# The second MLP's down product in Strassen blocks, with weight sums formed in the first MLP, in an fp32 decoder trunk

## The chip, the core and the metric

The kernel runs on one core of one Trainium2 chip. The metric is the device time of one execution in microseconds (us). The kernel before takes 2379.09 us (median of 3 runs, 2379.05 to 2379.59). The engines are PE (TensorE, matrix products), DVE (VectorE), ACT (ScalarE), POOL (GpSimd) and SP (SyncE, which here only starts transfers). Data moves between HBM and SBUF by 16 DMA engines; matrix products land in the eight banks of PSUM.

## What is computed

A trunk of two layers over 16 meta tokens and 256 tokens of width 2048, all in fp32: an RWKV-7 mixer, an MLP, gated linear attention (GLA), a second MLP, and a final norm over the 256 tokens. Only the MLPs and the norm matter here:

```python
def rms_norm(x, g, eps=1e-6):
    return x * lax.rsqrt(jnp.mean(x * x, axis=-1, keepdims=True) + eps) * g

def sq_relu_mlp(x, w1, w2):          # w1: 2048 x 8192, w2: 8192 x 2048
    h = jax.nn.relu(x @ w1)
    return (h * h) @ w2

# for each layer i
h = h + mix_out
h = h + sq_relu_mlp(rms_norm(h, norm_mlp[i]), mlp_w1[i], mlp_w2[i])
# at the end
return rms_norm(h, norm_f)[:, N_META:]
```

## The kernel before

The residual `hres` lies in SBUF feature by feature: 16 tiles of 128 features by 272 tokens. Every fp32 operand is cut into two reduced-precision halves, `hi` and `lo`, and a product is hi·hi + hi·lo + lo·hi. Weights come in chunks of 128x1024 (0.52 MB): SP loads a chunk into `raw`, ACT casts it to `hi` (L140), DVE subtracts to give `lo` (L141), and PE uses it for eight 128x128 blocks. In the MLPs one pool holds three `raw` and two each of `hi` and `lo`, so a chunk's `hi` can be written when PE is done with the chunk two before it.

An MLP (`mlp`) cuts its hidden width of 8192 into four quarters of 2048. `up(b)` makes the 16 rows of a quarter: two chunks each, a product over 16 blocks, then ReLU times the norm's factor (`z`, L272), a square (`s`) and the split into `h`. `down(b)` makes 16 rows of output from a quarter, again two chunks each, and adds them to `hres` (L213). The loop runs up(0), up(1), down(0), up(2), down(1), up(3), down(2), down(3). In the first MLP a product is three matmuls of 272 columns a block (`mm3`, L163 to L165). In the second, with 256 tokens, it is one of 512 columns (weight hi against hi and lo of the tokens) and one of 256 (weight lo against hi): `projws`, L196 and L197. The weights stand still in PE and the tokens stream.

A scheduler orders the instructions of each engine when the kernel is built; what is marked as high priority (the weight loads and their splits, by 2000 steps) is put as early as its buffers allow, and any other instruction goes into the first place at which the engine has nothing earlier in the program that it could do by the scheduler's own clock. The engines then execute in that built order. Parts under `manual_schedule` keep PE's order as written. The `x` tiles of the pool `xp` (16 of 128x2x272) hold operands of the mixers; during the first MLP they are free.

After the second MLP the final norm sums squares over the features with a matmul by ones, takes the factor, multiplies `hres` (already scaled by `norm_f`) and stores it feature by feature, five multiplications on DVE and one on POOL (L1328).

Of the kernel before, what the change touches and what calls it, by code (L numbers as in the profile page):

```python
# [10 lines left out]
F32 = mybir.dt.float32  # L11
F32R = mybir.dt.float32r
AF = mybir.ActivationFunctionType
ALU = mybir.AluOpType
# [16 lines left out]
NC4 = 4  # L31
DECAY = float(np.exp(-0.5))
NORM_EPS = 1e-6
# [21 lines left out]
class Kern:  # L55
# [203 lines left out]
    def mlp(self, layer, x, rstd, hres, off, done):  # L259
        nc, tc, ap = self.nc, self.tc, self.ap  # L260
        n = T - off
        w1, w2 = ap[f"mlp_w1_{layer}"], ap[f"mlp_w2_{layer}"]
        with ExitStack() as es:
            hp = es.enter_context(tc.tile_pool(name=f"hid{layer}", bufs=1, side="right", reuse_waits="tile"))

            def up(b):
                hid = []
                for f in range(KT):
                    src = [w1[b * KT + f, i] for i in range(2)]
                    ps = self.joined(hp, self.projw(src, x)) if n == SEQ else self.proj(src, x, n)  # L270
                    z = self.t(hp, [P, T], "z", 2)[:, :n]
                    nc.vector.scalar_tensor_tensor(out=self.two(z), in0=ps, scalar=0.0, in1=self.two(rstd), op0=ALU.max,  # L272
                                                   op1=ALU.mult)
# [4 lines left out]
                    nc.vector.tensor_tensor(out=ht[:, 1, :n], in0=s, in1=ht[:, 0, :n].bitcast(F32), op=ALU.subtract)  # L278
                    hid.append(ht)
                return hid  # L280

            def down(b, hid):
                for f in range(KT):
                    src = [w2[f, 2 * b + i] for i in range(2)]
                    one = n != SEQ or (b, f) == (NHB - 1, KT - 1)
                    self.addto(hres[:, f, off:], [self.proj(src, hid, n)] if one else self.projw(src, hid))
                    if b == NHB - 1:
                        done(f)

            hid = up(0)  # L290
# [4 lines left out]
            down(NHB - 1, hid)  # L295


    def rwkv(self, done):
# [691 lines left out]
        with tc.manual_schedule(engines={ENG.PE}):  # L990
# [5 lines left out]
            for g in range(2):  # L996
                last = nothing
                if g:
# [7 lines left out]
                    last = norm(1)  # L1006
                until(MARK[2 * g])
                some(inv, 99)
# [270 lines left out]
@with_exitstack  # L1279
def trunk(ctx, tc, ap):  # L1280
    K = Kern(ctx, tc, ap)
    nc = tc.nc
    out, hres = ap["out"], K.hres
    st = {}

    def operand(gname, off, pool):
        def f(kt):
            if kt == 0:
                p = pool()
                st["x"] = [K.t(p, [P, 2, T], "x", KT, F32R) for _ in range(KT)]  # L1290
                st["acc"] = K.t(K.sp, [P, T], "acc")
            with tc.high_priority(offset=3000) if kt == KT - 1 else ExitStack():
                K.prep(K.sp, kt, hres[:, kt, off:], gname, st["x"][kt], st["acc"], T - off)
        return f

    def x2():
        K.x2p = K.sp = ctx.enter_context(tc.tile_pool(name="x2", bufs=1, side="right", reuse_waits="tile"))
# [9 lines left out]
    def last(kt):  # L1307
        if kt == 0:
            st["acc"] = K.t(K.sp, [P, T], "acc")
        h = hres[:, kt, NMETA:]  # L1310
        if kt < KT - 1:
            K.sqacc(K.sp, kt, h, st["acc"], SEQ)
        else:
            st["sq"] = K.t(K.sp, [P, T], "sq")[:, :SEQ]
            nc.scalar.activation(st["sq"], h, AF.Square)  # L1315
        nc.scalar.mul(h, h, K.vec("norm_f", kt))

    fp = ctx.enter_context(tc.tile_pool(name="fin", bufs=1, side="right"))
    fin = K.t(fp, [P, KT - 2, SEQ], "fin")
    K.mlp(1, st["x"], rstd, hres, NMETA, last)  # L1320
    ss = K.pm()[:, :SEQ]
    for i, x in enumerate((st["acc"][:, :SEQ], st["sq"])):
        nc.tensor.matmul(ss, K.ones, x, start=i == 0, stop=i == 1)  # L1323
    rstd = K.rstd_from(K.sp, ss, SEQ, 1.0 / D, NORM_EPS, "acc")
    for a, b in ((0, 1), (14, 16), (1, 3), (3, 6), (6, 10), (10, 14)):
        h = hres[:, a:b, NMETA:]
        y = fin[:, a:b] if b < KT else h
        (nc.gpsimd if b == KT else nc.vector).tensor_tensor(out=y, in0=h, in1=rstd.unsqueeze(1).to_broadcast([P, b - a, SEQ]),  # L1328
                                                           op=ALU.mult)
        nc.sync.dma_start(out[:, a:b], y)  # L1330


def _tiles(w):
    k, f = w.shape
    return np.ascontiguousarray(w.reshape(k // 1024, 8, P, f // P, P).transpose(3, 0, 2, 1, 4)).reshape(
        f // P, k // 1024, P, 1024)


def _pad(w, cols):
# [82 lines left out]
```

## Time and profile before

| | |
|---|---|
| Median of three runs | 2379.09 us |
| Profiled execution: span from first to last instruction | 2375.3 us |
| Mean granted PE clock | 0.998 |
| Packets of the one queue that moves data (SP's) | 156784, 446.11 MB, 57.8% of 16 engines' span |
| First MLP, from its first matmul to its last | 590 to 1303 us |
| GLA | 1303 to 1692 us |
| Second MLP | 1692 to 2363 us |

The page gives no duration of the profiled execution other than its span; the median is 3.8 us longer. The span is the part that the trace explains. In groups of instructions, a matmul's duration is modelled and includes the time that it spends in the pipeline, so matmuls overlap; what one costs is the distance from its start to the next one's. The share of DMA is the mean busy share of the 16 DMA engines. Idle time of an engine says who was waited for (`<-`).

### The profile page before, as it was taken

How to read it: one execution, taken by the hardware profiler on the slowest of the kernel's cores; microseconds unless marked ns; L12 is line 12 of the kernel's file. 1: busy time of each engine (PE TensorE's matmuls, PEld its weight loads, DVE VectorE, ACT ScalarE, POOL GpSimd, SP SyncE). 2: the span in 40 equal slices, each digit the busy share in tenths (PEclk: the TensorE clock that was granted, in tenths of full speed). 3: DMA queues.
4: the chain of work that ended last, by engine and by line, in shares of the span. 5: the costliest groups of instructions: out<-in, count | busy, mean ns of one | idle time of the engine just before them, and what ended most of it. 6: DMA issues, size and time to landing. Idle time of an engine off the chain costs nothing. (4 is left out here: it accounts for less than half of the span.)

```text
span 2375.3 us, 48373 instructions
## 1 busy us (share of the span) xinstructions
PE 2344.9 (99%) x19849; PEld 2224.1 (94%) x19849; DVE 1607.3 (68%) x2701; ACT 1259.7 (53%) x2005; POOL 13.6 (1%) x38
## 2 busy tenths in 40 slices
PE   9999999999999999999999999999999999999998
PEld 8888888889999999999999999999999999999997
DVE  8869986848555555555556777767666666666666
ACT  6478645566555345345345556645555445445444
POOL 0000000000000000000000000000000000000000
PEclk9999999999999999999999999999999999999999
DMA  6469754535555555555555655456565666666664
GB/s 214 155 198 310 245 159 145 144 98 180 186 192 189 188 194 187 189 192 188 190 191 190 199 175 174 162 168 202 179 203 200 200 203 200 200 203 200 199 204 169
DMA packets 157005, 449.20 MB, mean 189 GB/s; under 512 B 33968, under 2 KB 49968, under 8 KB 156784
## 3 DMA queue, kind: packets, MB, share of 16 engines
q1 hardware_dynamic: 156784, 446.11, 57.8%
q8 instruction: 156, 2.56, 0.5%
q14 instruction: 65, 0.53, 0.1%
HBM read 429.93 MB, written 14.42 MB: 187 GB/s over the span
## 5 line engine op out<-in xcount | busy, mean ns | idle before, releaser
L141 DVE TENSOR_TENSOR lo<-raw,hi 128x1024 fp32r<-128x1024 f32 (+1 forms) x818 | 927.4, 1140 | 532.9 <-ACT hi L140 523.1
L140 ACT CAST hi<-raw 128x1024 fp32r<-128x1024 f32 (+1 forms) x818 | 794.2, 978 | 918.8 <-PE pj L164 519.4
L163 PE MATMUL pj<-x,hi 128*128 128x272 f32 (+1 forms) x2560 | 728.1, 284 | 1.6 <-DVE r L300 0.9
L165 PE MATMUL pj<-x,lo 128*128 128x272 f32 (+1 forms) x2560 | 714.8, 279 | 5.1 <-DVE lo L141 5.0
L164 PE MATMUL pj<-x,hi 128*128 128x272 f32 (+1 forms) x2560 | 713.8, 279 | 0.5 <-DVE x L240 0.5
L163 PEld LDWEIGHTS pj<-x,hi 128*128 128x128 f32 x2560 | 484.8, 189 | 14.1 <-issue 6.5
L165 PEld LDWEIGHTS pj<-x,lo 128*128 128x128 f32 x2560 | 484.9, 189 | 7.8 <-DVE lo L141 7.5
L164 PEld LDWEIGHTS pj<-x,hi 128*128 128x128 f32 x2560 | 485.0, 189 | 3.2 <-issue 1.4
L196 PE MATMUL pj<-x,hi 128*128 128x512 f32 x1280 | 419.8, 382 | 0.1
L197 PE MATMUL pj<-x,lo 128*128 128x256 f32 x1280 | 348.7, 273 | 0.0
L196 PE MATMUL pj<-h,hi 128*128 128x512 f32 x1008 | 330.3, 382 | 0.0
L163 PE MATMUL pj<-h,hi 128*128 128x272 f32 (+1 forms) x1040 | 290.1, 279 | 0.0
L164 PE MATMUL pj<-h,hi 128*128 128x272 f32 (+1 forms) x1040 | 290.1, 279 | 0.0
L165 PE MATMUL pj<-h,lo 128*128 128x272 f32 (+1 forms) x1040 | 290.1, 279 | 0.0
L197 PE MATMUL pj<-h,lo 128*128 128x256 f32 x1008 | 274.9, 273 | 0.1
L196 PEld LDWEIGHTS pj<-x,hi 128*128 128x128 f32 x1280 | 241.9, 189 | 33.9 <-DVE x L1088 0.4
L197 PEld LDWEIGHTS pj<-x,lo 128*128 128x128 f32 x1280 | 245.8, 192 | 0.1
L196 PEld LDWEIGHTS pj<-h,hi 128*128 128x128 f32 x1008 | 190.5, 189 | 26.5
L163 PEld LDWEIGHTS pj<-h,hi 128*128 128x128 f32 x1040 | 196.6, 189 | 0.0
L164 PEld LDWEIGHTS pj<-h,hi 128*128 128x128 f32 x1040 | 196.6, 189 | 0.0
L165 PEld LDWEIGHTS pj<-h,lo 128*128 128x128 f32 x1040 | 196.6, 189 | 0.0
L197 PEld LDWEIGHTS pj<-h,lo 128*128 128x128 f32 x1008 | 193.5, 192 | 0.4 <-DVE lo L141 0.4
(283 smaller groups left out, 2171.5 us busy)
## 6 DMA issues: line engine op xcount, KB each, us to landing
raw<-mlp_w_d SPq DMA_DIRECT2D x512, 512.0 KB, 3.4
raw<-gla_in_d SPq DMA_DIRECT2D x98, 512.0 KB, 3.4
raw<-w_rkv_d SPq DMA_DIRECT2D x80, 512.0 KB, 4.1
raw<-gla_o_d SPq DMA_DIRECT2D x32, 512.0 KB, 3.3
raw<-w_r_d SPq DMA_DIRECT2D x16, 512.0 KB, 3.4
raw<-rw_oQ_d SPq DMA_DIRECT2D x16, 512.0 KB, 3.4
raw<-lora_d SPq DMA_DIRECT2D x8, 512.0 KB, 3.7
raw<-rw_oA_d SPq DMA_DIRECT2D x8, 512.0 KB, 4.2
```

Source lines behind the costliest of these rows:

```text
L140: nc.scalar.copy(hi[:, h], raw[:, h])
L141: nc.vector.tensor_tensor(out=lo[:, h], in0=raw[:, h], in1=hi[:, h].bitcast(F32), op=ALU.subtract)
L163: nc.tensor.matmul(out, hi[:, ws], xh, start=first, stop=False)
L164: nc.tensor.matmul(out, hi[:, ws], xl, start=False, stop=False)
L165: nc.tensor.matmul(out, lo[:, ws], xh, start=False, stop=last)
L196: nc.tensor.matmul(wide, hi[:, ws], xt, start=kt == 0, stop=False)
L197: nc.tensor.matmul(one, lo[:, ws], xt[:, 0], start=False, stop=kt == nk - 1)
```

## The change

The first MLP's arithmetic and its PE order stay. Four things are new.

**Weight sums.** In the first MLP, `differences` forms three sums of 128x512 blocks of the second MLP's `w2` for 48 sets (4 quarters, 2 halves of the output width, 6 of 8 block rows) and stores them in HBM as `diff`. A set is three fetches by POOL's queue into free `x` tiles, three DVE instructions and three stores by POOL's queue. `paced` hands the steps out over 120 of the 128 rows of the first MLP, one call of `next(pre)` after each row.

**Strassen units.** The second product of the second MLP is turned round: tokens stand still in PE (128 hidden x 128 tokens), weights stream, 512 columns at a time. A unit is a block row p: 256 hidden, 256 tokens, 1024 outputs, or eight block products, of three matmuls each. In the six block rows of `FAST` they become seven products after Strassen (in Winograd's form), which need sums of the hidden blocks (four DVE additions of 128x128 for a pair of rows) and of the weights: a chunk of two `w2` blocks, one of two `diff` blocks, one of a block of each, and a 128x512 difference formed on the spot (`raw4`) with its own split. The eight products go to eight PSUM banks (`own`), which are emptied after the sixth fast row and in the plain rows.

**Order.** Rows of the first product alternate with units, in an order written by hand for PE. The pool `hid1` adds two more `raw`, `hi` and `lo`, used in turn with the old ones.

**Residual and norm.** `hres` is turned to token-by-feature form by 32 PE transposes beside the first eight rows (`htok`), the sums are added to it there, and the final norm works on it directly: squares with a running sum on ACT, factor per token, DVE and ACT scaling by quarters, eight stores.

```diff
+FAST = [0, 1, 2, 4, 5, 6]
...
                     hid.append(ht)
+                    next(pre, None)
...
+            if layer == 0:
+                pre = self.paced(self.differences(), 2 * NHB * KT - 8)
...
+    def differences(self):
...
+        def fetch(u):
...
+            for x, k in zip(held[u], (0, 3, 2)):
+                nc.gpsimd.dma_start(x, w[:, k])
+
+        def form(u):
+            x11, x12, x22 = held[u]
+            tt = nc.vector.tensor_tensor
+            tt(out=x22, in0=x22, in1=x12, op=ALU.subtract)
+            tt(out=x12, in0=x12, in1=x11, op=ALU.subtract)
+            tt(out=x11, in0=x11, in1=x22, op=ALU.add)
+
+        def store(u):
...
+            for x, k in ((t1, 0), (t3, 1), (t2, 2)):
+                nc.gpsimd.dma_start(self.diff[b, g, i][:, k], x)
+
+        def step(u):
+            if u >= 3:
+                store(u - 3)
+            if u < len(units):
+                fetch(u)
+            if 2 <= u < len(units) + 2:
+                form(u - 2)
...
+        def down(b, g):
...
+            def product(at, X, hi, lo, ws, last, first=False):
+                wh, wl, o = self.weave(hi[:, ws]), self.weave(lo[:, ws]), self.pairs(own[at])
+                nc.tensor.matmul(o, X[0], wh, start=first or at not in begun, stop=False)
+                nc.tensor.matmul(o, X[0], wl, start=False, stop=False)
+                nc.tensor.matmul(o, X[1], wh, start=False, stop=last)
...
+                    A = load([(both, w[:, :2])])
+                    B = load([(both, d[:, 1:])])
+                    E = load([(one, w[:, 2]), (two, d[:, 0])])
+                    with tc.high_priority(offset=2000):
+                        r4 = self.t(hp, [P, 512], "raw4", 1)
+                        tt(r4, A[0][:, two], B[0][:, two], ALU.subtract)
+                        G = split(hp, r4, 512)
...
+                    for i in (6, 7, 5, 2, 3, 4, 1) if p == 0 else (1, 6, 7, 5, 2, 3, 4):
+                        product(i, *todo[i], p == FAST[-1] and i in (1, 5, 6, 7))
...
+                unit = down(b, 0)
+                for f in range(10, 16):
+                    next(unit)
+                    up(b, f)
+                for _ in unit:
+                    pass
+                unit = down(b, 1)
+                for f in range(8):
+                    if b < NHB - 1:
+                        up(b + 1, f)
+                    next(unit)
+                for _ in unit:
+                    pass
```

Before each quarter's `down(b, 0)` ten of its rows are done, so each quarter has units 0 to 5 with a row behind each, units 6 and 7 without, then eight units with a row of the next quarter ahead of each; in the last quarter these eight have none.

What stands on DVE in the first MLP's first quarter, before. `lo` is the second half of a chunk, `z` and `h` belong to the 16 hidden rows:

```order
L141 TENSOR_TENSOR lo_8357<-raw_8354,hi_8356 128x1024
L272 SCALAR_TENSOR_TENSOR z_8346<-pj_8285,acc_8279 128x272
L141 TENSOR_TENSOR lo_8387<-raw_8384,hi_8386 128x1024
L278 TENSOR_TENSOR h_8350<-s_8348,h_8350 128x272
L141 TENSOR_TENSOR lo_8425<-raw_8422,hi_8424 128x1024
L272 SCALAR_TENSOR_TENSOR z_8414<-pj_8353,acc_8279 128x272
```

The same engine in the first MLP's second quarter, where the rows are the same, now (L143 is the old L141, L274 and L280 the old L272 and L278; L334 to L336 are the three instructions of a set, on `x` tiles that POOL fetched):

```order
L143 TENSOR_TENSOR lo_9438<-raw_9435,hi_9437 128x1024
L336 TENSOR_TENSOR x_12845<-x_12845,x_12847 128x512
L274 SCALAR_TENSOR_TENSOR z_9427<-pj_9366,acc_8282 128x272
L143 TENSOR_TENSOR lo_9468<-raw_9465,hi_9467 128x1024
L280 TENSOR_TENSOR h_9431<-s_9429,h_9431 128x272
L334 TENSOR_TENSOR x_12983<-x_12983,x_12982 128x512
L335 TENSOR_TENSOR x_12982<-x_12982,x_12981 128x512
L336 TENSOR_TENSOR x_12981<-x_12981,x_12983 128x512
L143 TENSOR_TENSOR lo_9518<-raw_9515,hi_9517 128x1024
L274 SCALAR_TENSOR_TENSOR z_9495<-pj_9434,acc_8282 128x272
L334 TENSOR_TENSOR x_13181<-x_13181,x_13180 128x512
L143 TENSOR_TENSOR lo_9548<-raw_9545,hi_9547 128x1024
```

Between two `lo` there now stand up to three instructions of a set. The scheduler has drawn the sets far ahead of the rows to which `paced` tied them: five stand before the first MLP's first `lo`s, the 6th to the 47th between the 3rd and the 64th of its 256 `lo`s, and the 48th near its end.

POOL's queue in the same stretch, now (it issued no transfer before); `w_d` is `w2`, and the numbers of the `x` tiles tell the sets apart:

```order
L329 DMA x_11005<-w_d 128x512
L329 DMA x_11006<-w_d 128x512
L329 DMA x_11007<-w_d 128x512
L342 DMA diff_8288<-x_10672 128x512
L342 DMA diff_8288<-x_10673 128x512
L342 DMA diff_8288<-x_10671 128x512
L329 DMA x_11141<-w_d 128x512
L329 DMA x_11142<-w_d 128x512
L329 DMA x_11143<-w_d 128x512
L342 DMA diff_8288<-x_10870 128x512
L342 DMA diff_8288<-x_10871 128x512
```

POOL alternates the fetches of a set with the stores of the set two or three before it. A store waits for DVE, and the fetches behind it wait with it.

DVE in the second MLP, before, one row of the first product after the other:

```order
L141 TENSOR_TENSOR lo_24817<-raw_24814,hi_24816 128x1024
L207 TENSOR_TENSOR cj_24781<-pj_24736,cj_24781 128x256
L272 SCALAR_TENSOR_TENSOR z_24784<-cj_24781,acc_21664 128x256
L141 TENSOR_TENSOR lo_24850<-raw_24847,hi_24849 128x1024
L278 TENSOR_TENSOR h_24788<-s_24786,h_24788 128x256
```

and now, beside rows that alternate with fast units (`raw_4084` and `lo_4086` are the difference formed on the spot and its `lo`, `F` and `HS` the sums of hidden blocks and their `lo`):

```order
L209 TENSOR_TENSOR cj_26379<-pj_22261,cj_26379 128x256
L409 SCALAR_TENSOR_TENSOR z_26382<-cj_26379,acc_22244 128x256
L356 TENSOR_TENSOR raw_4084_26508<-raw_26489,raw_26495 128x512
L356 TENSOR_TENSOR lo_26492<-raw_26489,hi_26491 128x1024
L356 TENSOR_TENSOR lo_26463<-raw_26460,hi_26462 128x1024
L356 TENSOR_TENSOR lo_26498<-raw_26495,hi_26497 128x1024
L356 TENSOR_TENSOR lo_4086_26511<-raw_4084_26508,hi_4085_26510 128x512
L356 TENSOR_TENSOR F_26296<-F_26296 128x128 x3
L356 TENSOR_TENSOR lo_26505<-raw_26501,hi_26504 128x1024
L356 TENSOR_TENSOR HS_26389<-F_26296,HS_26389 128x896
```

Where a row had two `lo` and three smaller instructions, a row with its unit now has five `lo`, two half-size instructions for the difference, and the sums of hidden blocks beside the smaller ones.

More of the change, by code (lines that the diff above doesn't have):

```diff
@@ L288, in down @@
                         done(f)
+                    next(pre, None)
+            pre = iter(())
+            if layer == 0:
+                pre = self.paced(self.differences(), 2 * NHB * KT - 8)
             hid = up(0)
@@ L295, in mlp, with operands, paced @@
             down(NHB - 1, hid)
+    def operands(self, b, g, p):
+        return self.ap["w2"][b, g, p]
+    def paced(self, steps, n):
+        steps = list(steps)
+        done = 0
+        for i in range(n):
+            while done < (i + 1) * len(steps) // n:
+                steps[done]()
+                done += 1
+            yield
+    def differences(self):
+        nc = self.nc
+        self.diff = self.t(self.dp, [NHB, 2, len(FAST), P, 3, 512], "diff")
+        units = [(b, g, i) for b in range(NHB) for g in range(2) for i in range(len(FAST))]
+        held = {}
+        def fetch(u):
+            b, g, i = units[u]
+            w = self.operands(b, g, FAST[i])
+            held[u] = [self.t(self.xp, [P, 2, T], "x", KT, F32R).bitcast(F32).rearrange("p s t -> p (s t)")[:, :512]
+                       for _ in range(3)]
+            for x, k in zip(held[u], (0, 3, 2)):
[7 more added lines that the diff above has]
+        def store(u):
+            b, g, i = units[u]
+            t2, t1, t3 = held.pop(u)
+            for x, k in ((t1, 0), (t3, 1), (t2, 2)):
[7 more added lines that the diff above has]
+                form(u - 2)
+        return [lambda u=u: step(u) for u in range(len(units) + 3)]
@@ L1296, in x2 @@
     def x2():
-        K.x2p = K.sp = ctx.enter_context(tc.tile_pool(name="x2", bufs=1, side="right", reuse_waits="tile"))
+        K.sp = ctx.enter_context(tc.tile_pool(name="sp", bufs=1, side="right", reuse_waits="tile"))
+        st["x2"] = ExitStack()
+        K.x2p = st["x2"].enter_context(tc.tile_pool(name="x2", bufs=1, side="right", reuse_waits="tile"))
         return K.x2p
@@ L1305, in trunk @@
     rstd = K.accstd(K.sp, st["acc"], SEQ)
[L1307 to L1330, printed above, removed]
+    st["x2"].close()
+    K.mlp1(st["x"], rstd)
 def _tiles(w):
@@ L1336, in _tiles, with _blocks @@
         f // P, k // 1024, P, 1024)
+def _blocks(w):
+    w = w.reshape(NHB, KT // 2, 2, P, 2, 2, 256, 2).transpose(0, 4, 1, 3, 2, 5, 7, 6).reshape(NHB, 2, KT // 2, P, 4, 512)
+    out = np.empty_like(w)
+    for p in range(KT // 2):
+        out[:, :, p] = w[:, :, p][..., [0, 2, 3, 1], :] if p in FAST else w[:, :, p]
+    return out
 def _pad(w, cols):
@@ L1415 @@
           for k, v in arr.items()}
-    ap["out"] = nc.dram_tensor("out_d", (P, KT, n), F32, kind="ExternalOutput").ap()
+    ap["out"] = nc.dram_tensor("out_d", (2, P, D), F32, kind="ExternalOutput").ap()
     with _tile.TileContext(nc) as tc:
@@ L1419 @@
     r = _run(nc, [{k + "_d": v for k, v in arr.items()}], core_ids=[0])
-    o = r.results[0]["out_d"].transpose(1, 0, 2).reshape(D, n).T
-    return np.ascontiguousarray(o)[None]
+    return np.ascontiguousarray(r.results[0]["out_d"]).reshape(1, n, D)
```

171 lines of the change are left out of this document (170 added, 1 removed).

## The prediction

> **What bounds the kernel now.** I read the page's busy times first, then a table by stretch for the two MLPs, then the order of time inside each.
>
> ```profile
> span 2375.3 us, 48373 instructions
> PE 2344.9 (99%) x19849; PEld 2224.1 (94%) x19849; DVE 1607.3 (68%) x2701; ACT 1259.7 (53%) x2005; POOL 13.6 (1%) x38
> ```
>
> TensorE (PE) is busy for 99% of the span, so a change gains what it takes off PE and loses every moment in which PE waits. POOL does next to nothing. The stretches below are: the first MLP, the second MLP, a piece of the second, and the two spells in which DMA worked hardest.
>
> ```profile
> core 0: us, PE busy (x) PEld busy (x) DVE busy (x) ACT busy (x) POOL busy (x), PEclk, DMA share, GB/s
> 590.00:1303.00 713.00, 712.50 (x6148) 712.17 (x6146) 405.93 (x483) 329.81 (x420) 0.00 (x0) 1.00 0.58 190
> 1692.00:2364.00 672.00, 671.72 (x4114) 617.30 (x4112) 441.08 (x590) 344.47 (x481) 0.00 (x0) 1.00 0.60 198
> 1800.00:2000.00 200.00, 200.00 (x1224) 183.81 (x1223) 131.13 (x176) 102.27 (x144) 0.00 (x0) 1.00 0.61 201
> 196.00:216.00 20.00, 19.77 (x174) 17.93 (x174) 18.02 (x45) 16.71 (x33) 1.07 (x3) 1.00 0.98 337
> 4.00:12.00 8.00, 6.47 (x23) 3.83 (x22) 4.35 (x11) 3.82 (x7) 0.00 (x0) 1.00 1.02 408
> ```
>
> Both MLPs are PE-bound at full clock (PEclk 1.00). In the first, VectorE (DVE) has 307 us to spare and the 16 DMA engines are busy for 0.58 at 190 GB/s. When all 16 are busy all the time they move 408 GB/s; a rate of 190 at a share of 0.58 would be 328 GB/s at full share. These two numbers decide the forecast.
>
> **PE work in the second MLP.** A pair of matmuls, 512 and 256 columns wide, in order of time:
>
> ```profile
> 1899.73 0.38 PE L196 MATMUL pj<-h,hi 128*128 128x512 f32 x1
> 1899.95 0.27 PE L197 MATMUL pj<-h,lo 128*128 128x256 f32 x1
> 1900.06 0.38 PE L196 MATMUL pj<-h,hi 128*128 128x512 f32 x1
> 2363.22 0.28 PE L165 MATMUL pj<-h,lo 128*128 128x256 f32 x1
> ```
>
> The second column is a modelled length; the cost is the distance between starts: 0.22 us for 512 columns, 0.11 for 256. The 200 us stretch has 1224 matmuls, 612 pairs, so 0.327 us a pair and, by thirds, 0.218 us for 512 columns. The second product now takes 63 x 16 pairs, 329.6 us, and a last row of 48 matmuls at 0.112 (5.4 us): 335.0 us. After, it is eight passes of six Strassen units (7 x 3 matmuls) and two plain ones (8 x 3), 174 matmuls each: 1392 x 0.218 = 303.5 us. The first product keeps its 1024 pairs. That is 31.5 us less. Added are 32 transposes of hres. The nearest row is
>
> ```profile
> L732 PE MATMUL pm<-cst,hres 128*64 128x128 f32 x128 | 9.2, 279 | 0.5 <-ACT hres L895 0.5
> ```
>
> whose 279 ns is again a length: 8.9 us at most; 128 columns at the rate above would be 1.8. I take 3.5, as lengths here run two to three times the distance. **PE: -28 us** (-30 to -23).
>
> **The end.** PE's last product ends near 2363.3, and 12 us follow, much of it the five multiplications and the last transfers:
>
> ```profile
> 2366.15 5.23 DVE L1328 TENSOR_TENSOR fin<-hres,acc 128x256 f32<-128x256 f32 x5 [2.19 <-ACT acc L232]
> 2366.20 1.50 POOL L1328 TENSOR_TENSOR hres<-hres,acc 128x512 f32<-128x512 f32 x1 [1867.29 <-ACT acc L232]
> 2366.66 0.34 SPq L1330 DMA_DIRECT2D out_d<-fin  x1
> 2368.27 3.47 SPq L1330 DMA_DIRECT2D out_d<-fin  x4
> ```
>
> After, one addition and one square (0.7 each) follow the last product, two tiny activations, then two DVE and two ScalarE (ACT) scalings side by side, 1.4 us, and transfers. I put it at 7 us: **-5 us** (-7 to 0).
>
> **Weight sums in the first MLP.** Each of 48 sets is three fetches, three DVE instructions and three stores, each of 128x512 fp32 (0.262 MB). The code paces them over 120 of 128 rows. The built order doesn't: of 48 sets, DVE's order holds the 6th to the 47th between the 3rd and the 64th lo of the first MLP, that is 42 sets in 61 chunks of weights out of 256. What a chunk takes:
>
> ```profile
> 902.53 1.05 ACT L140 CAST hi<-raw 128x1024 fp32r<-128x1024 f32 x1 [1.73 <-PE pj L164]
> 903.61 1.23 DVE L141 TENSOR_TENSOR lo<-raw,hi 128x1024 fp32r<-128x1024 f32 x1 [0.52 <-ACT hi L140]
> 904.75 0.44 DVE L278 TENSOR_TENSOR h<-s,h 128x272 fp32r<-128x272 f32 x1
> 905.31 1.05 ACT L140 CAST hi<-raw 128x1024 fp32r<-128x1024 f32 x1 [0.95 <-PE pj L164]
> ```
>
> From hi to hi it is 2.78 us, PE's time for 24 matmuls; 61 chunks are 169.6 us. There are two hi and two lo buffers, so PE can run one chunk ahead of DVE and no more. DVE executes in order: a set's first subtraction waits for its fetch, and behind it stand the next chunk's lo, and behind that PE.
>
> Bytes in these 61 chunks: 42 x 6 x 0.262 = 66.1 MB for the sets, 61 x 0.524 = 32.0 MB of weights, 98.1 MB. Off that come about three sets fetched ahead and three not yet stored (POOL's order puts the fetch of a set behind the store of the third one before it): 4.7 MB. The other 93.4 MB in 169.6 us would be 551 GB/s. At 408 they take 229 us (+59), at 328 they take 285 us (+115). POOL's transfers need the same 16 engines. With two queues full the rate should beat 328; the stretch from 196 us, full as well, speaks against 408 with its 337. I take 365: 256 us, **+86 us** (+59 to +115).
>
> The Trainium skill, "DMA: Bandwidth & Descriptors", section "Issuing engines are not separate DMA queues", says that transfers started from several engines run on the same 16 DMA engines and that this saves issue time alone; its section "Specifications" gives a ceiling of 435 GB/s, by which the term would be +45 us (an estimate). The trace shows 408 at a share of 1.02; no run here has a second queue.
>
> DVE alone would hardly bind:
>
> ```profile
> L141 DVE TENSOR_TENSOR lo<-raw,hi 128x1024 fp32r<-128x1024 f32 x690 | 845.0, 1225 | 520.0 <-ACT hi L140 511.3 <-DMA cad<-ca 2.1
> L141 DVE TENSOR_TENSOR lo<-raw,hi 128x512 fp32r<-128x512 f32 x128 | 82.4, 684 | 12.9 <-ACT hi L140 11.8
> L272 DVE SCALAR_TENSOR_TENSOR z<-pj,acc 128x272 f32<-128x272 f32 x64 | 28.3, 442 | 38.1 <-PE pj L165 38.0
> ```
>
> 61 x 1.225 + 30.5 x (0.44 + 0.44) + 42 x 3 x 0.684 = 188 us in 169.6: at most +18, less since neighbours overlap (904.75 starts 0.09 before 903.61 + 1.23 ends). It lies beside the DMA wait and is not added. Five sets stand before the first MLP, 15 instructions of 0.684: 0 to 10 us; I take **+4**.
>
> **Waits in the second MLP.** A Strassen unit needs three chunks and a 512-wide difference with its own hi and lo, where the same weights were two chunks. DVE, with the durations above (128x512: 0.684) and these:
>
> ```profile
> L272 DVE SCALAR_TENSOR_TENSOR z<-cj,acc 128x256 f32<-128x256 f32 x64 | 27.2, 425 | 2.2
> L207 DVE TENSOR_TENSOR cj<-pj,cj 128x256 f32<-128x256 f32 x64 | 26.7, 418 | 0.0
> ```
>
> 304 lo (372 us), 96 half-size (66), 64 x 0.84 for the rows (54), 96 additions of 512 (66), and the hidden sums, interpolated, about 59: 617 us beside PE's 642, where it was 441 in 672. For a row with a fast unit PE needs 16 x 0.327 + 21 x 0.218 = 9.8 us and DVE 10.5 by lengths, about 9.4 with overlap. 38 such pairs cost 0 to 25 us. The last eight units have no row beside them (PE 4.6 us each, DVE 4.9 to 6), nor have units 7 and 8 of each quarter's first pass: 5 to 35 us more, since behind a waiting lo stand the additions that empty the PSUM banks. I take **+22 us** (+5 to +60). The extra weights cost nothing beside that: 304 x 0.524 = 159 MB in 642 us are 248 GB/s, under 328, and PE's matmuls cover them.
>
> **Sum.** 2375.3 - 28 - 5 + 86 + 4 + 22 = 2454.3 us of span. The median shown is 3.8 us above the profiled span, which I add: **2458 us**, slower by 3.3%.
>
> **Rivals.**
> *The sums stay hidden* (faster). If they ran as paced, 75.5 MB over 713 us would add 106 to 190 GB/s, 296, under both rates, and 98 us of DVE fits in 307. Then 2379 - 33 + 22 = 2368, or 2351 if the second MLP waits for 5 us only. For it: the pacing in the code. Against it: DVE and POOL execute in their built order, 42 sets in 61 chunks. It decides if DMA can move 551 GB/s, or if the sets are not due so early. Chance 0.06, a part of it within 0.2%.
> *POOL's issue binds.* POOL issues no DMA before, so its price isn't shown. SyncE's issue is 0.34 us above, POOL's own instruction 1.50: six a set are 2.0 to 9.0 us, against 6.1 that the forecast has for a set and its chunks (256 / 42). Over 1.02 us each, POOL is the bound; at 1.25 a set takes 7.5 us, 315 us in all, +145, so 2517; at 1.5, 2580. Chance 0.15.
> *DVE locks POOL out.* Should an issue wait for a whole lo and a subtraction, 1.9 us, a set takes 11.4 us, +309: 2681. Chance 0.02. The Trainium skill, "SBUF — State Buffer", section "Who interferes with whom", describes such a lock against descriptors written by GpSimd, but infers that a two-input tensor_tensor doesn't hold it; no run here shows either.
> *The second MLP saturates DVE* beyond my +60, with the rest as forecast: about 2510. Chance 0.05.
>
> **How the numbers follow.** The forecast has 0.72. With all its terms at their good ends it gives 2379 - 37 + 59 + 5 = 2406, at their bad ends 2379 - 23 + 115 + 10 + 60 = 2541. The range 2405 to 2545 leaves out the hidden case, the lock and half of the POOL case. A measurement of this kernel tells 0.2% (5 us) from no change. Faster by more 0.05, within it 0.03, slower 0.92.
>
> **What would show it.** The first quarter or third of the first MLP should have DMA near a share of 1 at 330 to 410 GB/s, PE idle with lo named as releaser, and lo or a subtraction waiting for a transfer; the rest of that stage should run at 2.78 us a chunk. The stage should last about 800 us. If DMA stands below 0.8 there while POOL is busy, the POOL rival holds. The second MLP should have 512-wide matmuls 0.22 us apart, DVE over 85%, and last 655 to 670 us. The forecast is wrong if DMA moves over 450 GB/s, or if the sets wait for nothing.

## The result and the profile after

The changed kernel takes **2616.77 us** (median of 4 runs, 2613.74 to 2621.70), the one before 2379.27: a ratio of 1.1002, 95% interval 1.0987 to 1.1018. It is slower, as forecast, but by 237 us where 79 were forecast, and outside the range. The profiled execution took 2621.7 us with a span of 2619.9.

The page after: its first rows, then two of its rows by slices of 65 us (the granted clock in tenths of full speed, and what the DMA engines moved):

```profile
span 2619.9 us, 48317 instructions
PE 2413.9 (92%) x19205; PEld 2239.0 (85%) x19205; DVE 1832.4 (70%) x3025; ACT 1335.9 (51%) x2075; POOL 167.9 (6%) x325
PEclk9999999998999999999999999999998989989899
GB/s 210 154 234 281 220 137 160 88 248 351 393 391 382 229 190 191 189 192 187 192 200 206 178 168 163 171 200 199 198 198 199 202 165 215 200 182 196 186 209 159
```

PE was busy for 99% of the span and is now busy for 92%, though it has 644 instructions fewer; and its busy time has grown, because the granted clock is no longer full everywhere. The DMA rate stands out in four slices early in the first MLP. In the second MLP (the last third), where most of the time went, nothing stands out in it. The stages, each from the matmul that closes one norm to the one that closes the next, from the traces (the changed kernel's final norm has no such matmul, so there PE's last product ends the second MLP):

| stage, us | before | after | change | forecast |
|---|---|---|---|---|
| RWKV layer | 593.6 | 606.9 | +13.3 | +4 (sets ahead of the first MLP) |
| first MLP | 713.1 | 793.7 | +80.6 | +86 |
| GLA layer | 387.2 | 387.9 | +0.7 | 0 |
| second MLP | 670.9 | 819.4 | **+148.5** | **-6** (PE -28, waits +22) |
| end | 10.6 | 12.1 | +1.5 | -5 |
| span | 2375.3 | 2619.9 | +244.6 | +79 |

The table by stretch of the changed kernel (the part of the first MLP with the sets, the rest of it, the second MLP):

```profile
core 0: us, PE busy (x) PEld busy (x) DVE busy (x) ACT busy (x) POOL busy (x), PEclk, DMA share, GB/s
593.00:858.00 265.00, 211.44 (x1588) 204.83 (x1588) 190.67 (x279) 99.78 (x145) 136.30 (x253) 0.92 1.00 380
858.00:1408.00 550.00, 547.35 (x4719) 546.51 (x4718) 311.06 (x364) 245.38 (x300) 4.15 (x8) 1.00 0.59 195
1786.00:2608.00 822.00, 708.92 (x3475) 609.48 (x3474) 582.48 (x767) 415.06 (x541) 0.00 (x0) 0.93 0.59 193
```

The first row is what was forecast: DMA full, at 380 GB/s. The third is not: DVE is busy for 582 of 822 us (71%), ACT for 415, DMA for 0.59. No engine and no queue is full there, and still PE stands idle for 113 us. The matmul clock is 0.93, because it is halved for 119.5 us of this stage (41.0 us in the first MLP; 0 in both before). PE is busy in 105 of the 119.5 us, and at half rate half of that is lost. So 113 + 52 = 165 us of the second MLP is idleness and slow clock, most of the 177 us that it takes over the forecast 642 us of PE work.

The waits of the changed kernel in its second MLP that bear on loads, on the difference and on PE (engine, what it began late, the releaser; then us in total, times, the longest):

```profile
DVE lo L356 <- ACT hi L380: 127.0, 99, 4.5
ACT hi L380 <- DVE raw L356: 82.5, 32, 8.2
ACT hi L380 <- DMA raw<-mlp_w_d: 53.4, 21, 6.4
PE pj L448 <- DVE cj L209: 37.9, 10, 4.5
DVE raw L356 <- DMA raw<-w_d: 37.2, 16, 4.3
PE pj L405 <- DVE cj L209: 29.5, 12, 4.2
```

They form a ring. DVE waits for ACT's hi, ACT for a subtraction of DVE (`raw`, the difference formed on the spot), and that for a load. And a load is issued the moment DVE gives a buffer back, as the rows of the SyncE queue say:

```profile
SPq L374 <- DVE lo L356: 485.7, 205, 12.0
SPq L374 <- DVE cj L209: 110.0, 48, 3.0
```

What such a wait does to PE, at one place: a plain unit of the third quarter, in order of time on ACT, DVE and PE.

```profile
2240.33 1.04 ACT L380 CAST hi<-raw 128x1024 fp32r<-128x1024 f32 x1 [2.76 <-DMA raw<-mlp_w_d]
2241.28 0.37 ACT L208 COPY cj<-pj 128x256 f32<-128x256 f32 x1
...
2241.40 1.23 DVE L356 TENSOR_TENSOR lo<-raw,hi 128x1024 fp32r<-128x1024 f32 x1 [0.22 <-ACT hi L380]
2242.55 0.68 DVE L356 TENSOR_TENSOR htok<-htok,hres 128x512 f32<-128x512 f32 x1
2243.15 0.42 DVE L209 TENSOR_TENSOR cj<-pj,cj 128x256 f32<-128x256 f32 x1
...
2240.09 0.38 PE L450 MATMUL pu<-hi,HC 128*128 128x512 f32 x1
2243.62 0.79 PE L448 MATMUL pj<-hi,HC 128*128 128x512 f32 x1 [3.16 <-DVE cj L209]
2244.21 0.63 PE L449 MATMUL pj<-lo,HC 128*128 128x512 f32 x1
2244.64 0.63 PE L450 MATMUL pj<-hi,HC 128*128 128x512 f32 x1
```

A load is late by 2.76 us. The copy that empties PE's bank `pj` needs nothing of that load, but it stands behind the cast that does, and `cj` stands behind two more instructions of DVE. PE, which wants `pj` for product 0, stops for 3.16 us. Then its 512-wide matmuls start 0.43 us apart instead of 0.22, until about 2249.7: the clock has halved.

### The profile page after: what moved, and what is told of

It reads as the page before. It is cut to its first block, busy times and chain, and to the rows that moved or that the text cites. A ratio compares the mean times of both kernels' runs of the same rounds, so it can differ in the third digit from the quotient of the medians.

```text
span 2619.9 us, 48317 instructions
## 1 busy us (share of the span) xinstructions
PE 2413.9 (92%) x19205; PEld 2239.0 (85%) x19205; DVE 1832.4 (70%) x3025; ACT 1335.9 (51%) x2075; POOL 167.9 (6%) x325
## 5 line engine op out<-in xcount | busy, mean ns | idle before, releaser
L142 ACT CAST hi<-raw 128x1024 fp32r<-128x1024 f32 (+1 forms) x562 | 526.2, 947 | 638.8 <-PE pj L166 494.4
L143 DVE TENSOR_TENSOR lo<-raw,hi 128x1024 fp32r<-128x1024 f32 (+1 forms) x562 | 613.2, 1100 | 286.5 <-ACT hi L142 282.6
L380 ACT CAST hi<-raw 128x1024 fp32r<-128x1024 f32 (+1 forms) x352 | 339.3, 986 | 313.7 <-DVE raw L356 82.5
L356 DVE TENSOR_TENSOR lo<-raw,hi 128x1024 fp32r<-128x1024 f32 (+1 forms) x352 | 394.5, 1148 | 130.0 <-ACT hi L380 129.0
L405 PE MATMUL pj<-x,hi 128*128 128x512 f32 x896 | 323.0, 406 | 46.4 <-DVE cj L209 29.5
L165 PE MATMUL pj<-h,hi 128*128 128x272 f32 x1024 | 285.8, 279 | 1.0 <-ACT hi L142 1.0
L167 PE MATMUL pj<-h,lo 128*128 128x272 f32 x1024 | 285.9, 279 | 0.8 <-DVE lo L143 0.8
L166 PE MATMUL pj<-h,hi 128*128 128x272 f32 x1024 | 285.7, 279 | 0.0
L406 PE MATMUL pj<-x,lo 128*128 128x256 f32 x896 | 257.0, 287 | 5.1 <-DVE lo L356 4.9
L165 PEld LDWEIGHTS pj<-h,hi 128*128 128x128 f32 x1024 | 193.5, 189 | 1.2 <-ACT hi L142 1.2
L167 PEld LDWEIGHTS pj<-h,lo 128*128 128x128 f32 x1024 | 193.5, 189 | 1.1 <-DVE lo L143 1.0
L166 PEld LDWEIGHTS pj<-h,hi 128*128 128x128 f32 x1024 | 193.5, 189 | 0.0
L342 POOL DMA_DIRECT2D diff<-x x144 | 78.3, 545 | 534.6 <-DVE x L334 464.4
L329 POOL DMA_DIRECT2D x<-w_d x144 | 77.9, 542 | 129.7 <-DMA diff<-x 56.4
```

Of the source, the lines that this page charges most:

```text
L142: nc.scalar.copy(hi[:, h], raw[:, h])
L143: nc.vector.tensor_tensor(out=lo[:, h], in0=raw[:, h], in1=hi[:, h].bitcast(F32), op=ALU.subtract)
L165: nc.tensor.matmul(out, hi[:, ws], xh, start=first, stop=False)
L166: nc.tensor.matmul(out, hi[:, ws], xl, start=False, stop=False)
L167: nc.tensor.matmul(out, lo[:, ws], xh, start=False, stop=last)
L329: nc.gpsimd.dma_start(x, w[:, k])
```

## The experiments

Sixteen runs follow, each of one execution but for the last; the kernel before took 2377 to 2381 us beside them. "Second MLP" and the other names are the stages of the table above. Where the code of a stage stayed as it was, the stage still moved: the second MLP took 812 to 823 us in the runs that left it alone and 833 and 834 in the two that read `w2` in place of `diff` in it, the first MLP 789 to 797. So a difference of less than 10 us between two runs says little. First, which part of the change costs what.

**No weight sums.**

```diff
-            if layer == 0:
-                pre = self.paced(self.differences(), 2 * NHB * KT - 8)
-                    d = self.diff[b, g, FAST.index(p)]
+                    d = w[:, 1:]
```

> Left out: the weight sums of the first MLP; the second MLP reads blocks of w2 in place of diff, in the same sizes and number. Theory (the sums cost what the first MLP and the stage before it gained, 81 + 13 us, and the second MLP's loss is its own): the first MLP back at 713 us, the second unchanged at 819 +-10, the whole near 2616 - 94 = 2522 us. Rival (the two losses belong together, for instance by where diff lies in HBM): the second MLP falls by more than 20 us too.

2545.94 us. The first MLP is back at 713.8 us and the RWKV layer at 595.7, so the sums cost 80 + 11 us there. The second MLP takes 833.9 us. That is 14 us more than in the changed kernel, outside the 10 that were expected, and not less. Its loss is its own: it doesn't come from the sums, from where they lie in HBM or from anything that the first MLP leaves behind.

**The sets' transfers without their arithmetic.**

```diff
-            if 2 <= u < len(units) + 2:
-                form(u - 2)
```

> Left out: the three DVE instructions of each set; fetches and stores stay, so diff holds plain blocks. Theory (PE lost time because DVE, in its built order, stood before a set's transfer with the next lo behind it): the transfers run as fast as the engines let them, nobody on DVE waits, the first MLP is 713 to 735 us and the whole 2530 to 2550. Rival (the transfers themselves starve the weight loads of DMA): the first MLP stays above 770 us.

2575.61 us; first MLP 751.5, between the two theories. The transfers alone cost 38 us of that stage, though DMA is just as full. A stretch of 50 us in this run, where PE is busy for 46 of them:

```profile
700.00:750.00 50.00, 45.95 (x377) 44.04 (x376) 25.03 (x31) 22.73 (x32) 24.89 (x46) 1.00 1.02 407
```

The same stretch of the changed kernel has PE busy for 41 and a clock of 0.93:

```profile
700.00:750.00 50.00, 40.95 (x312) 39.73 (x312) 36.99 (x52) 18.49 (x25) 27.05 (x51) 0.93 1.02 395
```

So full DMA engines are half of the loss in the first MLP. The other half needs DVE's subtractions, which wait for fetches with the next `lo` behind them. In the changed kernel, from 590 to 870 us:

```profile
DVE x L334 <- DMA x<-w_d: 59.8, 31, 4.9
PE pj L167 <- DVE lo L143: 52.0, 28, 4.7
```

**The sets held back to their rows.** A small copy on POOL makes each fetch wait for the row to which `paced` tied it.

```diff
+                    self.mark = s[:, :4]
...
+                    self.mark = hres[:, f, off : off + 4]
...
+                nc.gpsimd.tensor_copy(x[:, :4], self.mark)
                 nc.gpsimd.dma_start(x, w[:, k])
```

> Before each fetch POOL copies four columns of the row just made into the tile that is fetched, which ties each set to its row; the built order then has 48 sets over 220 of 256 chunks. Theory (42 sets in 61 chunks asked for 551 GB/s): about 296 GB/s, DMA under a share of 0.9, the first MLP at 713 to 730 us, the whole near 2616 - 85 = 2530. Rival (each set costs its wait wherever it stands, some 2 us): the first MLP stays above 770 us.

2782.57 us; first MLP 969.5 and halved clock for 174 us of it. Slower still, by 176 us of that stage. The fetches now come row by row, but on DVE the subtraction of a set is still placed where the scheduler took its data to be there. In this trace one `lo` or none starts between the last fetch of a set and its first subtraction. In the first MLP:

```profile
DVE x L337 <- DMA x<-w_d: 186.5, 48, 4.9
PE pj L167 <- DVE lo L143: 168.3, 49, 4.8
```

Each of the 48 sets stops DVE for about 4 us, and PE stops with it.

**The subtractions held back as well.** A value of a later row goes into the first of the three instructions as a scalar, so that DVE's order has a set two steps behind its fetch.

```diff
+            tick = self.t(self.tp, [P, 1], "tick", 2)
+            nc.vector.tensor_scalar(out=tick, in0=self.mark[:, :1], scalar1=0.0, scalar2=1.0, op0=ALU.mult, op1=ALU.add)
-            tt(out=x22, in0=x22, in1=x12, op=ALU.subtract)
+            nc.vector.scalar_tensor_tensor(out=x22, in0=x22, scalar=tick, in1=x12, op0=ALU.mult, op1=ALU.subtract)
```

> As the paced kernel, and a set's first subtraction multiplies by a 1.0 made from the row of two steps later, so that it stands some nine chunks behind the row that its fetch is tied to. Latency theory (the paced kernel lost 4 us on DVE per set, because the build put each subtraction a chunk or two behind a fetch that takes 7.7 us to land, and PE's clock halved behind each stop): no wait for transfers, the first MLP at 715 to 745 us. Rival (DVE's own work in a full order stops PE): above 800 us.

2618.46 us; first MLP 804.6. DVE's waits for fetches are gone, and with them the loss of the run before; still the stage is 11 us longer than in the changed kernel. What is waited for now, in the first MLP, is weights:

```profile
ACT hi L142 <- DMA raw<-mlp_w_d: 181.5, 57, 5.1
PE pj L167 <- DVE lo L143: 32.8, 45, 0.9
```

By its number the run meets the rival (above 800 us), and the two runs that follow ask whether by its cause too. The theory that DVE's wait was the cause left something open: six transfers of a set are issued one after the other, and a load of weights in among them may be late.

**DVE's arithmetic without the transfers.**

```diff
-            for x, k in zip(held[u], (0, 3, 2)):
-                nc.gpsimd.dma_start(x, w[:, k])
...
-            for x, k in ((t1, 0), (t3, 1), (t2, 2)):
-                nc.gpsimd.dma_start(self.diff[b, g, i][:, k], x)
```

> Fetches and stores of the sets are left out, and the second MLP reads blocks of w2 in place of the weight sums; the three DVE instructions of each set stay, on tiles that hold zeros, each set tied to its row as in e8_late. It asks what DVE's work costs by itself: with the transfers alone the first MLP took 751.5 us, with neither 713.8, with both and tied late 804.6. Theory A (DVE's work alone is harmless, DVE has 300 us to spare, and only transfers and what waits for them stop PE): first MLP 713 to 725 us, no half clock. Theory B (the instructions of a set stand ahead of a chunk's lo, PE stops once for most sets and its clock halves behind each): over 750 us.

First MLP 714.0 us, no half clock:

```profile
595.00:1309.00 714.00, 712.90 (x6148) 712.22 (x6147) 500.31 (x672) 329.72 (x420) 0.00 (x0) 1.00 0.59 190
```

DVE does 94 us more than before (500.3 against 405.9) and PE loses nothing, as theory A has it: DVE's work, spread over the stage, is not what e8_late lost. No run has this work without its transfers as the changed kernel has it, 42 sets in 61 chunks; the prediction put at most 18 us on that.

**The same work dealt in single pieces.** As e8_late, and the nine pieces of a set go out one fetch, one instruction and one store at a time.

```diff
-        return [lambda u=u: step(u) for u in range(len(units) + 3)]
+        return [lambda u=u, j=j: part(u, j) for u in range(len(units) + 3) for j in range(3)]
```

> As e8_late, but the nine pieces of a set (three fetches, three DVE instructions, three stores) are handed out one piece of each kind at a time, so that about two or three transfers are issued for a row in place of six at once. Theory A (the weight loads come late because they stand behind bursts of six transfers): first MLP under 760 us, ACT's waits for loads well under the 181.5 us of e8_late. Theory B (it is the sum of the bytes and of DVE's work, however they are dealt): 785 us or more.

2544.85 us; first MLP **735.9**, no half clock, with all bytes and all arithmetic in it:

```profile
594.00:1329.00 735.00, 723.51 (x6140) 714.48 (x6140) 499.40 (x672) 330.34 (x419) 227.35 (x432) 1.00 0.85 287
```

and of its waits:

```profile
ACT hi L142 <- DMA raw<-mlp_w_d: 126.9, 61, 3.4
```

The loads are still late 61 times, but by 3.4 us at most and not 5.1, which the chunks in hand nearly cover: PE is idle for 11.5 us of this stretch where it was for 54 of e8_late's 804. Bursts it was, and the sums so dealt cost 22 us of the first MLP, not 80.

Now the second MLP, where 177 us are to be explained.

**Four raw buffers in the second pool.**

```diff
-                raw = self.t(pool, [P, 1024], "raw", self.raw_bufs if pool is self.wp else 2)
+                raw = self.t(pool, [P, 1024], "raw", self.raw_bufs if pool is self.wp else 4)
```

> The pool of the second MLP holds four raw buffers instead of two (and one fsq instead of two, for the space). Supply theory (a raw buffer turns in 8 us or more, load 4.4 to 4.8 us and split, so two in every second place feed a chunk each 2 us at best, and ACT and DVE stand before loads with PE's evacuations behind them): the second MLP falls from 819 us by 60 us or more. Rival, bank theory (PE stands in the plain units because rows and product 0 share one PSUM bank): it falls by less than 25 us.

2564.29 us; second MLP 766.2, so 53 us less, near the 60 of the supply theory and well over the 25 of its rival.

**Other banks for the plain units.** The two plain units go to the end of each pass, and their product 0 to a bank that no row uses.

```diff
-FAST = [0, 1, 2, 4, 5, 6]
+FAST = [0, 1, 2, 3, 4, 5]
...
+                    spare = 7 if last else 1
-                            product(i, (H
+                            product(i or spare, (H
```

> The fast units are the block rows 0 to 5, the plain ones 6 and 7, and product 0 of the plain units goes to banks 1 and 7, which are empty by then, so that no unit uses the bank of the rows. Bank theory (PE waited 38 us in ten plain units for cj, and the clock halves behind such waits): the second MLP falls from 819 us by 50 us or more. Supply theory (the evacuation is late because ACT and DVE stand before loads): by less than 25 us, as the waits come back at other products.

2578.97 us; second MLP 777.6, 42 us less, between the two theories. PE's wait of 37.9 us in the plain units' `pj` is gone. The rows' own wait for `cj` has grown from 29.5 us in 12 waits:

```profile
PE pj L405 <- DVE cj L209: 49.5, 20, 4.2
```

Moving the plain units has also changed the order on the other engines. ACT's wait for the difference formed on the spot was 82.5 us in 32 waits, and is now

```profile
ACT hi L380 <- DVE raw L356: 33.8, 29, 2.5
```

so the 42 us are not shown to be the bank's alone.

**Both, with the sums held back.** The edits of e8_late, e5_banks and e4_raw4 in one kernel.

> The late sums, the free banks and the four raw buffers in one kernel. If the gains add up: 2616 - 70 for the sums, - 53 for the buffers, - 20 to - 60 for the banks, 2430 to 2475 us; the second MLP at 700 to 750. If buffers and banks cure the same wait, the second MLP stays near 760.

2514.74 us; second MLP 719.2, so 100 us less: the gains of e4_raw4 and e5_banks add up (53 + 42). The whole is slower than the 2430 to 2475 us expected, because the late sums alone save nothing in the first MLP (800.1 us).

**The difference in its turn.**

```diff
-                    with tc.high_priority(offset=2000):
+                    with ExitStack():
                         r4 = self.t(hp, [P, 512], "raw4", 1)
```

> The changed kernel with the difference formed on the spot, its hi and its lo at ordinary priority in place of ahead of all else; nothing is left out. Theory A (ACT's hi of the difference, and the ordinary hi behind it, wait for a DVE subtraction that itself waits for two loads: 82.5 us in 32 waits of ACT): second MLP 780 us or less against 819.4. Theory B (the order doesn't matter, the buffers do: a raw buffer comes free too late whoever waits for it): 805 us or more.

2586.74 us; second MLP 784.5, 35 us less, between the two theories and near the first. ACT's wait for the subtraction is 34.8 us instead of 82.5, longest 2.8 instead of 8.2:

```profile
ACT hi L380 <- DVE raw L356: 34.8, 28, 2.8
```

**Two chunks a unit.** Neither the third chunk nor the difference, so their work on SyncE, ACT and DVE goes as well; PE's matmuls stay.

```diff
-                    B = load([(both, d[:, 1:])])
+                    B = A
...
-                        tt(r4, A[0][:, two], B[0][:, two], ALU.subtract)
-                        G = split(hp, r4, 512)
+                    G = E
```

> Changed computation: a fast unit loads two chunks, as a plain unit does, and its products take the blocks of these two in place of the second diff chunk and of the difference formed on the spot, both left out. PE's work stays. Supply theory: the second MLP falls to 660 to 720 us, what is left being the shared bank. Bank theory: it stays above 780 us.

2473.32 us; second MLP **676.7**, so 143 of the 177 us hang on the third chunk and the difference.

```profile
1784.00:2460.00 676.00, 647.03 (x3457) 574.59 (x3458) 475.33 (x620) 339.95 (x443) 0.00 (x0) 0.99 0.62 197
```

PE is busy for 647.0 us, 5.1 of it lost to 10.2 us of half clock: 642 us, the forecast for PE's work. The Strassen products save what they should.

**The third chunk's work without its load.**

```diff
-                    B = load([(both, d[:, 1:])])
+                    with tc.high_priority(offset=2000):
+                        B = split(pool, A[0], 1024)
```

> The changed kernel without the transfer of a fast unit's second chunk (the two weight sums x21-x22 and the other one that unit products 7 and 6 read): its hi and its lo are formed a second time from the first chunk, so that ACT's and DVE's work and the difference on the spot stay, and 0.524 MB and one raw buffer a unit go. Taking the chunk and the difference away with all their work brought the second MLP from 819.4 to 676.7 us. Theory A (supply: the loads and the raw buffers they wait for): under 720 us. Theory B (ACT's and DVE's added work and its order): over 780 us.

2557.70 us; second MLP 756.2: both theories missed. 63 us of the 143 hang on the load and its raw buffer, and on the subtraction's waiting for one load in place of two; the other 80 on the hi, lo and difference that remain. How much of the 80 is their order and how much the work itself, this run doesn't say.

**All the milder forms at once**: e10_spread_transfers, e5_banks, e4_raw4 and e11_difference_in_turn in one kernel; then timed.

> All the milder forms at once: the pieces of the sets spread as in e10_spread_transfers, the two plain units put last in each pass and their product 0 in another PSUM bank as in e5_banks, four raw buffers in the second pool as in e4_raw4, and the difference at ordinary priority. Nothing is left out. If the gains add up: first MLP under 760 us, second MLP under 700 us, in all about 2440 us, still slower than before (2379). If the first MLP stays at 800 us: about 2500 us.

> The kernel of e12_spread_banks_buffers once more, timed in rounds against the kernel before, for an interval: 2443.6 us in its one look, so a ratio of 1.027 to the kernel before, 1.025 to 1.029 expected. It computes all of the reference.

2443.58 us in the first run, 2443.61 (2440.34 to 2445.85) as the median of four more: a ratio of 1.0272 to the kernel before, interval 1.0255 to 1.0289. In the profile of e16_milder_timed the first MLP takes 741.5 us, the second 705.8 with 23.9 us of half clock, a little more than the 700 expected. Busy times of the page, then the second MLP:

```profile
PE 2353.9 (96%) x19205; PEld 2189.8 (90%) x19205; DVE 1834.8 (75%) x3073; ACT 1327.0 (54%) x2075; POOL 239.9 (10%) x469
```

```profile
1724.00:2429.00 705.00, 663.78 (x3456) 575.83 (x3457) 574.35 (x765) 406.59 (x540) 0.00 (x0) 0.98 0.69 225
```

It is 173 us faster than the changed kernel with nothing left out, by order, banks and buffers alone: 114 of the 177 us of the second MLP were not the work's price. It beats the changed kernel and not the one before. What is left in its second MLP is 64 us over 642.

**The same without the third load, and without the difference.** As in e13_no_third_load; and with `G = E` as in e6_two_chunks, but with all three loads.

> e12_spread_banks_buffers with the same chunk left unloaded, its hi, its lo and the difference kept. There the second MLP still took 706.7 us, with PE's own work at about 642. Theory A (what is left there is the supply of the third chunk): 670 us or less. Theory B (it is DVE's and ACT's work in their order): 695 us or more.

> e12_spread_banks_buffers with all three loads, but without the difference formed on the spot, its hi and its lo; product 4 reads the third chunk's half instead. Theory A (what is left there hangs on the chain of two loads, subtraction, hi, lo, product 4): 675 us or less for the second MLP. Theory B (on the three loads and their hi and lo): 695 us or more.

2440.97 and 2417.30 us; second MLP 699.7 and 679.7. The load is worth 7 us now (theory B), no more than such runs differ by; the difference with its hi and lo 27 (a little short of theory A). In the first of the two the subtraction waits for one load in place of two, so the second load is not what makes the difference dear either. So supply is settled; the subtraction with its hi, its lo and product 4 is what remains, and some 38 us that no run took apart.

## Why the prediction was wrong

**The failing step** is "Waits in the second MLP": "I take **+22 us** (+5 to +60)." It measured 819.4 - 642 = +177. The step added up busy times, DVE's 617 us beside PE's 642, and priced what neighbouring instructions would collide. DVE's busy time came out at 582, so the count was fair and the question wrong: PE lost its time to waits while every engine had room. The runs put in its place, for the changed kernel: 63 us for the third chunk's load and the raw buffer that it waits for (e13_no_third_load; four buffers give 53); 80 us for the added hi, lo and difference in an order in which one late operand holds up instructions that don't need it (e13_no_third_load against e6_two_chunks); 35 us beside these. That order and buffers are at fault for most of it, and not the amount of work, e16_milder_timed shows: the same loads, casts and subtractions, 114 us less. The edits of banks (42) and priority (35) overlap with those parts and aren't to be added to them. The sentence "The extra weights cost nothing beside that", which rested on 248 GB/s against 328, is wrong by the 63 us: bandwidth was there (0.59 of DMA), free buffers were not.

**A cost that the forecast didn't have** is the halved clock: 160 us at half rate in the two MLPs. PE was busy in 143 of them, so some 71 us were lost, three tenths of the whole. It is a surcharge on stops: e10_spread_transfers has none of it in the first MLP, e3_paced has 174 us.

**Weight sums, +86 with +4 ahead of the first MLP**: 80.6 + 13.3 = 94 us, right in size, though the 13.3 lie above the 0 to 10 allowed. DMA was full (share 1.00, 380 GB/s against the 365 taken) from 593 to 858 us, 265 us against 256 forecast, and the rest of the stage ran clean at 195 GB/s. But the reason was half right, and the size came out partly by luck. "It lies beside the DMA wait and is not added" of DVE's work falls: with DMA just as full and no subtractions the first MLP lost 38 us, not 81 (e2_no_subtractions). Full DMA engines alone leave PE 92% busy; a DVE that stops for a fetch with a chunk's `lo` behind it, and the clock that halves, made the other half. DVE's work by itself, spread over the stage, costs nothing (e9_only_subtractions, +0.9 us).

**PE, -28**: right, 642 us by e6_two_chunks. **The end, -5**: counted as the prediction did, from PE's last product, it got no shorter, 12.1 us against 12.0 (the table's 10.6 starts at the norm's matmul); no run was spent on it.

**The rivals.** That the sums stay hidden was tied to "if the sets are not due so early". That alone makes it worse (e3_paced); with the subtractions late and the transfers spread it comes within 22 us of true (e10_spread_transfers), and the total is slower all the same, for the second MLP. POOL's issue doesn't bind:

```profile
L342 POOL DMA_DIRECT2D diff<-x x144 | 78.3, 545 | 534.6 <-DVE x L334 464.4 <-DMA x<-w_d 29.2 <-DMA diff<-x 9.9
L329 POOL DMA_DIRECT2D x<-w_d x144 | 77.9, 542 | 129.7 <-DMA diff<-x 56.4 <-DVE r L566 43.5 <-DMA x<-w_d 25.8
```

0.54 us an issue is 3.3 us a set against the 6.1 from which it would have decided; these rows speak against the lock as well, since an issue that waited out a `lo` and a subtraction would show the 1.9 us forecast for it, and the longest of the 288 took 0.68. That the second MLP would lose more than 60 us had 0.05, and named the wrong cause: DVE is at 71%, not saturated, where the prediction looked for over 85%. None of the rivals was a ring of waits through loads, buffers and two queues that run in order, and that was the case.

## What to carry to other kernels

Where PE has no slack, don't price an added operand by the busy time of the engines that prepare it. Count the buffers through which it comes, and write down what stands behind it on each engine: a load that was 3 us late held up the instructions behind it on ACT and DVE, whether they needed it or not, and PE paid for the first that it did need. Deal side work out in single pieces, tied to rows of the main work at both its transfers and its arithmetic; the same bytes and subtractions cost 81 us in the first MLP as built, 91 tied to rows in bursts and 23 in pieces.

## What the runs showed of the hardware

**The clock halves behind a window in which PE stood for more than about 2 us.** From the first MLP on, the changed kernel's trace has 29 stops of PE of 2.5 us or more, and a spell of half rate begins at or right behind 27 of them; of 13 stops of 1.5 to 2.5 us, at 8; of 38 of 0.3 to 1.5 us, at 2. In the two MLPs 23 spells last 3.41 us and 12 last 6.83, and all begin on one grid of 3.41 us. So do the spells of every other run here, each on a grid of its own. Cut along that grid, from the first MLP to PE's last product, the traces of all runs show 323 windows at full rate in which PE stood for more than 2.02 us, and half rate follows every one; of the 1390 with less than 1.6 us none is followed by it; of the 132 between, 35 are. The changed kernel's two long stops without a spell (3.67 us up to 1889.75, 3.21 us up to 1916.87) lie across a line of the grid, with less than 2 us on either side. A stop of 3 us within one window costs PE nearer 5 to 6 (an estimate: half of the 3.41 or 6.83 us behind it is lost as well). In e16_milder_timed 52 of 59 stops are under 1.5 us, and 24 us of its second MLP run at half rate where 119.5 did.

**With the DMA engines full, every transfer takes over 7 us to land, whoever issues it.** The changed kernel's transfers from 607 to 857 us, from issue to landing (median us last):

```profile
raw<-mlp_w_d SPq DMA_DIRECT2D x62, 512.0 KB, 7.2
diff<-x POOLq DMA_DIRECT2D x123, 256.0 KB, 7.4
x<-w_d POOLq DMA_DIRECT2D x115, 256.0 KB, 7.8
```

The loads of weights took 3.4 us in the first MLP before, and 4.3 in the changed kernel behind that stretch. Half the bytes land no sooner there. In e3_paced, where POOL's fetches come row by row, they take 5.1 us, nearly two chunks of the first MLP (2.78 us each), so a subtraction that stands one `lo` behind its last fetch is early.
